# A streaming encoder layer on one core: scores of two heads in turns, a block's closing carried into the next block, stage buffers in another order

## The chip, the cores and the metric

The kernel runs on one core of one Trainium2 chip. The metric is device microseconds of one execution. Five engines work side by side, each through its own list of instructions in order: TensorE (PE, matrix products; its weight loads are counted apart as PEld), VectorE (DVE), ScalarE (ACT), GpSimd (POOL), and SyncE (SP), which here only issues transfers. Matrix products land in PSUM, eight banks, from which DVE or ACT must copy ("evict") them; the other tiles live in SBUF.

## The reference

One layer of an encoder, width 1024, for 2048 prompt tokens and 32 sample tokens. Each of three parts is wrapped as `x = x + rmsnorm(part(rmsnorm(x)))`:

1. one projection `h @ w_in`, whose columns feed a band attention with 8 heads (each 64-token chunk sees itself and 8 chunks before it) and a gated linear attention with 4 heads, key width 64 and value width 128; both outputs go through `w_o`;
2. cross-attention, 4 heads of 256, to 256 memory tokens;
3. a feed-forward block of width 2816.

The lines that matter here:

```
ob, sp = gla_recurrence(qb, kb, vb, la, s0, GLA_BLOCK)   # 4 heads, decay per key channel
def swiglu(h, w_gate, w_up, w_down):
    return (jax.nn.silu(h @ w_gate) * (h @ w_up)) @ w_down
```

## The kernel before

Matrix products are done to near float32 precision with two-part operands: a value is split into a rounded part (`ACT.copy` to float32r, line 77) and a remainder (a subtraction on DVE or POOL, line 81), and a product takes three matmuls (`mm3`, line 136). Projections and the gate and up products use a scheme with seven instead of eight block products (`seven_mov`, `seven_sta`); X, Y and Z are its three output banks.

The program is written in stages, each in its own set of pools: the projections (to about 625 us), attention and linear attention with the output projection (to about 1590), cross-attention (to about 2030), and the feed-forward stage (to the end). SBUF addresses follow the order in which a stage opens its pools, so a new stage's tile must wait until the tiles of the stage before at the same addresses are no longer used.

**What sets the order.** The code names engines and data. A planner then orders every engine's instructions: it goes through a simulated time and gives a free engine the ready instruction with the lowest number. The number is the place in the program text, less an offset inside `tc.high_priority(offset=...)`. `PRI` is 4000; weights are loaded and split at `PRI`. The order is then fixed, and an engine that waits holds all behind it.

**Linear attention (`gla_tile`).** One tile of 128 tokens at a time, 16 tiles and one of 32 sample tokens. Per pair of heads `f`, exponentials of the decays are put into `W`; then each head `e` of the pair (partitions 0 to 63 or 64 to 127) gets 15 products of 64x64 in one PSUM bank (`sps`, lines 922 and 926; the profile calls it `g_s`), which ACT (927) and DVE (928) evict. Two banks (`pm`) serve all of linear attention. The 15 products of a head are issued together, then its eviction, then the next head.

**Cross-attention.** Five blocks of 416 tokens. `mem_out` multiplies by `w_mo` into `y`, `mem_fin` closes: statistic, scaling by `g_post_mem` (1347), residual (1348), write to `x2d`, a second statistic, scaling by `g_pre_ffn` (1352), write to `h2d`. For the last block `mem_fin` runs at twice `PRI`, and the residual's additions alternate between POOL and DVE.

**Feed-forward stage.** Three blocks `b`, each with two column halves `ci` of 348 or 346 tokens. `ffn_raw` loads the input `hr` from `h2d`, `ffn_ops` makes the seven operands `mf` (in `mps[0..6]`). A block has 11 groups `g`. `gate_up(g)` makes two units, gate and up, of seven products with 12 matmuls each, and the result `u`; `down([g-1])` follows, 16 products of 6 matmuls, half 1 first, added by DVE into `acc[ci]` (1510, 183). `acc` has two buffers, `u` three, `sg` five, the output banks `pd` six. In group 8 the next block's input is loaded, in group 10 its operands are made. After group 10, `finish(ci)` closes each half: statistic (1534), Ln and Exp on ACT (85, 86), eight multiplications on DVE (1541), eight residual additions on POOL (183), two loads (1525) and two writes (1544). Both calls stand at the end of the block, ahead of the next block's text:

```
down([NF // 2 - 1], [held])
for ci in (1, 0):
    finish(ci, lambda kh: stage(f"x2r{b}_{ci}_{kh}"))
```

The evictions of `unit` and `down` have no priority of their own; in the projection stage a helper `out` gives evictions twice `PRI`.

Of the kernel before, what the change touches and what calls it, by code (L numbers as in the profile page):

```python
# [45 lines left out]
def encoder_step(ctx, tc, ins, outs):  # L46
# [171 lines left out]


    lo_set[0] = [POOL, DVE]  # L220
    WCH = 1056
    with ExitStack() as ph:
# [136 lines left out]

        def out(f, *a):  # L360

            with tc.high_priority(offset=2 * PRI):
                f(*a)
# [236 lines left out]
    with ExitStack() as ph:  # L600
# [257 lines left out]
        def gla_tile(tk, n, st, name):  # L858
# [53 lines left out]
            for f in range(2):  # L912
                W = Ws[f]
                for e in range(2):
                    h = 2 * f + e
                    rs = slice(e * 64, e * 64 + 64)
                    kf, qf = kq[rs, f, 0], kq[rs, f, 1]
                    ms = gp.tile([P, 7, 64], F32, tag="ms", name=f"{name}_ms{h}")
                    sps = pm.tile([P, 8, 64], F32, tag="gla", name=f"{name}_s{h}")
                    at = at_p[h]  # L920
                    if n == P:
                        PE.matmul(sps[0:64, 7, :], lhsT=W[rs, 1, 0:64], rhs=W[rs, 1, 64:128], start=True, stop=True)
                        for li in range(7):
                            for bk in (slice(0, 64), slice(64, 128)):
                                lh, rh = (W[rs, 2 + li, bk], W[rs, 2 + li, bk]) if li < 6 else (kf[:, bk], qf[:, bk])
                                PE.matmul(sps[bk, li, :], lhsT=lh, rhs=rh, start=True, stop=True)
# [7 lines left out]
                    else:  # L934
                        for li in range(6):
                            lh, rh = (W[rs, 3 + li, :n], W[rs, 3 + li, :n]) if li < 5 else (kf[:, :n], qf[:, :n])
                            PE.matmul(sps[:n, li, :n], lhsT=lh, rhs=rh, start=True, stop=True)
# [278 lines left out]
    with ExitStack() as ph:  # L1216
# [121 lines left out]
        def mem_fin(b, y):  # L1338
            s, n = CB[b]
            last = b == len(CB) - 1  # L1340
            with tc.high_priority(offset=2 * PRI if last else 0):
# [15 lines left out]
        out = []  # L1357
        for b in range(len(CB)):
            mo, heads = mem_attn(b)
            fill = [partial(mem_q, b + 1, mv, m) for m in range(KT)] if b + 1 < len(CB) else out  # L1360
# [4 lines left out]
            out = mem_out(b, mo)  # L1365
            if b != len(CB) - 2:
                for it in out:
                    it()
# [5 lines left out]
    with ExitStack() as ph:  # L1374
# [88 lines left out]
        for b, (s, n) in enumerate(CF):  # L1463
# [219 lines left out]
```

## Time and profile before

| | |
|---|---|
| median of 3 runs | 3535.33 us (3531.69 to 3543.06) |
| profiled execution | 3536.25 us |
| its span | 3534.5 us |
| PE busy | 3254.4 us (92%) |
| DVE, ACT, POOL busy | 2279.1, 1699.5, 1528.3 us |
| mean granted TensorE clock | 0.951 |

Span is the time from the first to the last instruction; the profiled execution lies some microseconds around it. Busy times are sums over the span; an engine's busy matmul time includes matmuls at a lowered clock. In the timeline a row gives start, length, engine, line, operation, tiles written and read, and the number of instructions merged; a bracket gives the idle time before it and what ended it. In rows of groups the two numbers behind the bar are busy time and the mean of one in nanoseconds. Rows of waits give the total, the number of times and the longest. A merged row of overlapping matmuls ends when the last one does.

### The profile page before, as it was taken

The numbers are of one execution on the slowest core, as the hardware profiler recorded it, in microseconds if no ns is written. First come the engines' busy times: TensorE is split into PE (matmuls) and PEld (weight loads), VectorE is DVE, ScalarE is ACT, GpSimd is POOL, SyncE is SP. The second block draws the span as 40 slices with busy tenths as digits, with TensorE's granted clock in tenths as the row PEclk, the third lists the DMA queues.
The fourth block names the chain that finished last, engine by engine and source line by source line (L and its number), as shares of the span: only waits on it lengthen the run. The fifth ranks groups of instructions, "written<-read, shape, count | busy, mean of one in ns | idle before, by whom it ended". The sixth has DMA issues, their size and how long they took to land.

```text
span 3534.5 us, 58393 instructions
## 1 busy us (share of the span) xinstructions
PE 3254.4 (92%) x21387; PEld 3092.7 (87%) x21387; DVE 2279.1 (64%) x4089; ACT 1699.5 (48%) x3716; POOL 1528.3 (43%) x1331
## 2 busy tenths in 40 slices
PE   7788899899999798879999879999989999899998
PEld 7787899788888577879899869999889999899998
DVE  6774855575676666265566766666876666866665
ACT  4554545556665465345455443333443334443334
POOL 4543533353445544653434453333453334543332
PEclk8999999999999798999999979999999999999999
DMA  5448364877585565963655552222342222322222
GB/s 140 155 129 284 105 185 132 260 233 230 177 276 169 188 190 176 295 210 120 212 190 178 155 159 80 72 72 72 94 136 83 72 72 84 100 86 82 72 72 89
DMA packets 520112, 520.42 MB, mean 147 GB/s; under 512 B 81936, under 2 KB 450745, under 8 KB 519825
## 3 DMA queue, kind: packets, MB, share of 16 engines
q1 hardware_dynamic: 519825, 516.70, 47.2%
q8 instruction: 168, 2.75, 0.3%
q14 instruction: 119, 0.97, 0.1%
HBM read 386.82 MB, written 130.87 MB: 146 GB/s over the span
## 4 chain that ended last, share of the span: by engine, by line
PE 64%; DVE 9%; DMA 6%; POOL 3%; ACT 3%; issue 2%; SPq 1%; POOLq 0%; DVEq 0%; ACTq 0%
PE pdn L136 13%; PE pg_X L136 7%; PE pu_X L136 6%; PE wops L989 4%; PE mops L136 4%; PE pg_Y L136 3%; PE pu_Y L136 3%; PE po L715 2%; PE mqps L136 2%; PE pg_Z L136 2%; PE pu_Z L136 2%; PE s L710 1%; PE ms L136 1%; PE pt L742 1%; PE mpv L136 1%
## 5 line engine op out<-in xcount | busy, mean ns | idle before, releaser
L136 PE MATMUL pdn<-u,wd 128*128 128x346 f32 (+1 forms) x3168 | 527.9, 324 | 11.3 <-DVE up L183 9.8
L136 PEld LDWEIGHTS pdn<-u,wd 128*128 128x128 f32 x3168 | 512.0, 191 | 13.8 <-DVE up L183 10.4
L77 ACT CAST wg_s<-wg_r 128x512 fp32r<-128x512 f32 x231 | 139.6, 620 | 420.7 <-PE pdn L136 194.1
L136 PE MATMUL pu_X<-mf,wu_s 128*128 128x346 f32 (+1 forms) x1584 | 280.7, 323 | 11.4 <-DVE up L183 11.4
L136 PE MATMUL pg_X<-mf,wg_s 128*128 128x346 f32 (+1 forms) x1584 | 283.9, 329 | 7.7 <-DVE mf L81 3.3
L183 DVE TENSOR_TENSOR acc<-acc,pdn 128x346 f32<-128x346 f32 (+1 forms) x464 | 231.4, 512 | 87.3 <-PE pdn L136 87.2
L136 PEld LDWEIGHTS pg_X<-mf,wg_s 128*128 128x128 f32 x1584 | 265.0, 195 | 10.5 <-DVE mf L81 4.2
L136 PEld LDWEIGHTS pu_X<-mf,wu_s 128*128 128x128 f32 x1584 | 258.2, 190 | 12.2 <-issue 12.2
L81 POOL TENSOR_TENSOR wu_s<-wu_r,wu_s 128x512 fp32r<-128x512 f32 x132 | 175.9, 1333 | 212.7 <-ACT wu_s L77 208.5
L81 POOL TENSOR_TENSOR wg_s<-wg_r,wg_s 128x512 fp32r<-128x512 f32 x99 | 136.2, 1376 | 292.9 <-ACT wg_s L77 292.9
L989 PE MATMUL wops<-om,wo_s 128*128 128x512 f32 (+1 forms) x960 | 217.9, 378 | 23.9 <-ACT wo_s L77 10.3
L81 POOL TENSOR_TENSOR u<-sg,u 128x346 fp32r<-128x346 f32 (+1 forms) x132 | 135.4, 1037 | 193.1 <-ACT u L77 193.1
L136 PE MATMUL mops<-mo,wmo_s 128*128 128x416 f32 x960 | 199.0, 359 | 14.4 <-ACT mo L1318 6.5
L989 PEld LDWEIGHTS wops<-om,wo_s 128*128 128x128 f32 x960 | 163.8, 204 | 53.3 <-ACT wo_s L77 11.1
L136 PEld LDWEIGHTS mops<-mo,wmo_s 128*128 128x128 f32 x960 | 179.6, 191 | 20.4 <-ACT mo L1318 7.5
L77 ACT CAST wu_s<-wu_r 128x512 fp32r<-128x512 f32 x231 | 136.4, 618 | 70.7 <-DVE wu_r L183 36.0
L715 PE MATMUL po<-prt,v 128*128 128x128 f32 x1120 | 161.9, 290 | 7.9 <-ACT prt L744 5.6
L136 PE MATMUL mqps<-m,wmq_s 128*128 128x416 f32 x768 | 163.1, 362 | 5.1 <-DVE wmq_s L81 5.1
L715 PEld LDWEIGHTS po<-prt,v 128*128 128x128 f32 x1120 | 149.0, 203 | 15.8 <-ACT prt L744 6.3
L81 DVE TENSOR_TENSOR wg_s<-wg_r,wg_s 128x512 fp32r<-128x512 f32 x132 | 97.9, 742 | 90.5 <-ACT wg_s L77 89.1
L136 PEld LDWEIGHTS mqps<-m,wmq_s 128*128 128x128 f32 x768 | 145.0, 194 | 8.5 <-DVE wmq_s L81 5.8
L136 PE MATMUL pg_Y<-mf,wg_s 128*128 128x346 f32 (+1 forms) x792 | 139.5, 325 | 8.9 <-ACT mf L77 5.7
(478 smaller groups left out, 7964.2 us busy)
## 6 DMA issues: line engine op xcount, KB each, us to landing
wg_r<-in_w_ffn_gate_dram SPq DMA_DIRECT2D x66, 512.0 KB, 4.3
wu_r<-in_w_ffn_up_dram SPq DMA_DIRECT2D x66, 512.0 KB, 4.1
wd_r<-in_w_ffn_down_dram SPq DMA_DIRECT2D x66, 512.0 KB, 3.4
wmq_r<-in_w_mq_dram SPq DMA_DIRECT2D x80, 256.0 KB, 2.9
wmo_r<-in_w_mo_dram SPq DMA_DIRECT2D x80, 256.0 KB, 3.1
q<-qd SPq DMA_DIRECT2D x32, 512.0 KB, 5.4
wo_r<-in_w_o_dram SPq DMA_DIRECT2D x64, 256.0 KB, 4.3
om<-od SPq DMA_DIRECT2D x24, 512.0 KB, 7.3
```

Of the source, the lines that this page charges most:

```text
L77: ACT.copy(hi, src)
L81: lo_eng.tensor_tensor(out=lo, in0=src, in1=hi.bitcast(F32), op=ALU.subtract)
L136: PE.matmul(ps, lhsT=a, rhs=b, start=first and i == 0, stop=last and i == len(seq) - 1, skip_group_check=skip)
L183: eng.tensor_tensor(out=out, in0=a, in1=b, op=ALU.add)
L710: PE.matmul(ps_out, lhsT=q[:, 2 * i + e, q0 : q0 + nq], rhs=ks[:, e, k0 : k0 + ncol], start=i == 0, stop=i == 1)
L715: PE.matmul(po[:, e * P : e * P + n], lhsT=v[:kk, j, e * 64 : e * 64 + P], rhs=prt[:kk, j, :n], start=j == 0, stop=j == len(rows) - 1)
L742: PE.transpose(ptp[:kk, j, :n], pr[:n, c0 : c0 + kk], ident[:n, :n])
L989: PE.matmul(ps, lhsT=a, rhs=b, start=i == 0, stop=i == len(seq) - 1)
```

## The change

Three edits. In `gla_tile` the 15 products of the two heads of a pair are issued in turns, head by head within each product, into two banks; the evictions of both follow. In the feed-forward stage all evictions of `unit` and `down` go through `out` (twice `PRI`), which moves to where all stages see it, and `finish` of a block that is not the last is no longer called at its end but kept in `late`: half 1 is closed behind `gate_up(0)` of the next block, half 0 behind `gate_up(1)`. At the change from cross-attention the last `mem_fin` loses its priority, `ffn_raw(0)` and `ffn_ops(0)` get `PRI`, and the feed-forward pools are opened in another order, raw and split weights in pools of their own (`cwr`, `cws`), so that other tiles lie over those of cross-attention. No arithmetic is added or removed.

```diff
-                for e in range(2):
-                    h = 2 * f + e
-                    rs = slice(e * 64, e * 64 + 64)
-                    kf, qf = kq[rs, f, 0], kq[rs, f, 1]
+                hs = [(2 * f + e, slice(e * 64, e * 64 + 64), pm.tile([P, 8, 64], F32, tag="gla", name=f"{name}_s{2 * f + e}")) for e in range(2)]
+                if n == P:
+                    for h, rs, sps in hs:
+                        PE.matmul(sps[0:64, 7, :], lhsT=W[rs, 1, 0:64], rhs=W[rs, 1, 64:128], start=True, stop=True)
+                    for li in range(7):
+                        for bk in (slice(0, 64), slice(64, 128)):
+                            for h, rs, sps in hs:
+                                lh, rh = (W[rs, 2 + li, bk], W[rs, 2 + li, bk]) if li < 6 else (kq[rs, f, 0, bk], kq[rs, f, 1, bk])
+                                PE.matmul(sps[bk, li, :], lhsT=lh, rhs=rh, start=True, stop=True)
...
+                for h, rs, sps in hs:
                     ms = gp.tile([P, 7, 64], F32, tag="ms", name=f"{name}_ms{h}")
...
         def mem_fin(b, y):
             s, n = CB[b]
             last = b == len(CB) - 1
-            with tc.high_priority(offset=2 * PRI if last else 0):
+            if True:
...
-        mps = {i: pool(f"cm{i}", 1) for i in (5, 6)}
+        mps = {i: pool(f"cm{i}", 1) for i in (5, 6, 4)}
         gp = pool("cg", 4)
-        wp = pool("cw", 4)
+        wr = pool("cwr", WRB)
+        mps.update({i: pool(f"cm{i}", 1) for i in (0, 1)})
+        up_ = pool("cp", 3)
+        sp = pool("cs", 4)
+        mps.update({i: pool(f"cm{i}", 1) for i in (3, 2)})
+        ws = pool("cws", WSB)
+        np_ = pool("cn", 1)
         uu = pool("cu", UB)
-        sp = pool("cs", 4)
-        mps.update({i: pool(f"cm{i}", 1) for i in (4, 0, 1, 2, 3)})
-        up_ = pool("cp", 3)
-        np_ = pool("cn", 1)
         xp = pool("cx", 2)
...
             prod(X, w[0], m[0], True, True)
-            ACT.copy(cp[0], X)
+            out(ACT.copy, cp[0], X)
...
             prod(Y, w[3], m[3], False, True)
-            add(DVE, dst[0, 1], cp[2], Y)
+            out(add, DVE, dst[0, 1], cp[2], Y)
...
-        ops = ffn_ops(0, ffn_raw(0))
+        with tc.high_priority(offset=PRI):
+            ops = ffn_ops(0, ffn_raw(0))
+        late = []
...
                         if gs[0] == 0:
-                            DVE.tensor_copy(acc[ci][:, m, :n], ps[:, :n])
+                            out(DVE.tensor_copy, acc[ci][:, m, :n], ps[:, :n])
                         else:
-                            add(DVE, acc[ci][:, m, :n], acc[ci][:, m, :n], ps[:, :n])
+                            out(add, DVE, acc[ci][:, m, :n], acc[ci][:, m, :n], ps[:, :n])
...
                 u = gate_up(g, last and g == NF // 2 - 1)
+                if late:
+                    late.pop(0)()
...
                 down([NF // 2 - 1], [held])
-                for ci in (1, 0):
-                    finish(ci, lambda kh: stage(f"x2r{b}_{ci}_{kh}"))
+                late = [partial(finish, ci, lambda kh, nm=f"x2r{b}_{ci}": stage(f"{nm}_{kh}")) for ci in (1, 0)]
```

More of the change, by code (lines that the diff above doesn't have):

```diff
@@ L217, in seven_sta, with out @@
         put(a22)
+    def out(f, *a):
+        with tc.high_priority(offset=2 * PRI):
+            f(*a)
     lo_set[0] = [POOL, DVE]
@@ L1356, in encoder_step @@
         mv = mem_h(1)
-        out = []
+        proj = []
         for b in range(len(CB)):
             mo, heads = mem_attn(b)
-            fill = [partial(mem_q, b + 1, mv, m) for m in range(KT)] if b + 1 < len(CB) else out
+            fill = [partial(mem_q, b + 1, mv, m) for m in range(KT)] if b + 1 < len(CB) else proj
             for it in weave(heads, fill, lead=QLEAD):
@@ L1364, in encoder_step @@
                 mv = mem_h(b + 2)
-            out = mem_out(b, mo)
+            proj = mem_out(b, mo)
             if b != len(CB) - 2:
-                for it in out:
+                for it in proj:
                     it()
@@ L1428, in put @@
                 def put(q):
-                    w = wp.tile([P, 2, HK, P], F32R, tag="wsp", name=f"{name}_s{len(ops)}", bufs=WSB)
+                    w = ws.tile([P, 2, HK, P], F32R, tag="wsp", name=f"{name}_s{len(ops)}", bufs=WSB)
                     split(w[:, 0], w[:, 1], raw[q])
@@ L1528, in spare, with finish @@
                 return mps[i].tile([P, KT, 348], F32, tag="mov", name=name)
-            def finish(ci, xrs):
+            def finish(ci, xrs, b=b, s=s, n=n, acc=acc, ssqs=ssqs, last=b == len(CF) - 1, load_x2=load_x2):
                 a = acc[ci]
```

33 lines of the change are left out of this document (13 added, 20 removed).

## The prediction

> **What bounds the kernel now.** I read the page first: its busy times, the slices and the chain of work that ended last.
>
> ```profile
> span 3534.5 us, 58393 instructions
> PE 3254.4 (92%) x21387; PEld 3092.7 (87%) x21387; DVE 2279.1 (64%) x4089; ACT 1699.5 (48%) x3716; POOL 1528.3 (43%) x1331
> PE   7788899899999798879999879999989999899998
> PEclk8999999999999798999999979999999999999999
> PE 64%; DVE 9%; DMA 6%; POOL 3%; ACT 3%; issue 2%; SPq 1%; POOLq 0%; DVEq 0%; ACTq 0%
> ```
>
> PE is the bound, and what it can still give lies in the dips of its row. I therefore asked next for the busy time of each engine in stretches cut at the stage changes: the linear-attention stage, the passage from cross-attention to the feed-forward blocks, a quiet part of a feed-forward block, and the two places where one feed-forward block follows another. The columns are stretch, length, busy time (instructions) of PE, PEld, DVE, ACT and POOL, then granted clock, DMA share and GB/s.
>
> ```profile
> 625.00:1590.00 965.00, 861.76 (x6798) 752.01 (x6795) 593.84 (x1551) 538.79 (x1421) 462.80 (x541) 0.92 0.69 219
> 2030.00:2110.00 80.00, 51.53 (x235) 46.75 (x236) 57.60 (x67) 34.64 (x56) 44.28 (x24) 0.77 0.52 166
> 2110.00:2490.00 380.00, 380.00 (x2391) 380.00 (x2391) 230.72 (x389) 147.43 (x291) 142.56 (x117) 1.00 0.25 76
> 2490.00:2620.00 130.00, 112.12 (x655) 109.75 (x654) 115.81 (x144) 64.89 (x113) 72.74 (x50) 0.92 0.43 131
> 2978.00:3108.00 130.00, 112.30 (x655) 109.93 (x654) 115.80 (x145) 65.01 (x114) 72.24 (x50) 0.92 0.36 109
> ```
>
> In the quiet part PE never rests: 380/2391 = 0.159 us per matmul. At that rate the 655 matmuls of each block change need 104.1 us, and take 130: 25.9 us lost, twice. The 235 of the passage need 37.3 us and take 80: 42.7 us lost. Together 94.5 us; nothing is to be had inside a block.
>
> **The change, part by part.**
>
> *Evictions put first (`out` in `unit` and `down`).* In the quiet part there is no idle PE to remove, so they are worth nothing there; at a block change PE's waits and timeline show what they meet.
>
> ```profile
> PE pu_Z L136 <- ACT wu_s L77: 6.4, 1, 6.4
> PE pu_X L136 <- DVE up L183: 5.7, 1, 5.7
> PE pdn L136 <- DVE up L183: 4.9, 1, 4.9
> 2511.06 6.97 PE L136 MATMUL pdn<-u,wd 128*128 128x348 f32 x24 [4.93 <-DVE up L183]
> 2554.22 6.12 DVE L1541 SCALAR_TENSOR_TENSOR acc<-acc,g_post_ffn,n_r 128x348 f32<-128x348 f32 x6 [2.34 <-ACT n_r L86]
> 2579.98 8.73 DVE L1541 SCALAR_TENSOR_TENSOR acc<-acc,g_post_ffn,n_r 128x348 f32<-128x348 f32 x8 [2.25 <-ACT n_r L86]
> 2588.64 0.50 DVE L183 TENSOR_TENSOR up<-pu_c,pu_Y 128x346 f32<-128x346 f32 x1
> ```
>
> Three stops, 17.0 us. In two of them DVE works through a run of the closing's multiplications (6.12 and 8.73 us, 1.09 each) while an eviction (`up`) or a weight's subtraction stands behind; in the first it prepares the next block's input. The rest of the 25.9 us is clock: after the 4.93 us stop, 24 matmuls took 6.97 us where 0.159 each makes 3.8, so 3.2 us more. The Trainium skill ("TensorE: Matmul & The Clock Gate", Part 1) says that a window of about 3.4 us without work halves the clock and as long a busy one restores it. The trace agrees in kind; by the page's figures a stop would cost only 1.7 us beyond itself, and the sum below would be 3 us lower.
>
> With evictions ahead of everything, what stands before one is a single running instruction, about 2 us at most.
>
> *The closing moved (`late`).* Nothing is added or removed: per column half one statistic matmul, ACT's Ln and Exp with their table loads, 8 DVE multiplications, 8 POOL additions, two loads and two writes. But the half 1 closing now ranks behind group 0 of the next block, half 0's behind group 1, and the next block's `acc` buffers (two, one per half) are the ones being closed. What is late next is therefore the first write of `acc`, in the first `down`. From the end of the old block PE has groups 0 and 1 (168 matmuls each, 26.7 us), half 1 of `down` (48, 7.6 us) and six banks of half 0 (36, 5.7 us): 66.7 us, then it stands. Half 0's closing, step by step:
>
> ```profile
> 2575.53 0.75 PE L1534 MATMUL n_ps<-ssq,ones 128*128 128x348 f32 x2
> 2576.30 1.28 ACT L85 ACT_TABLE_LOAD   x1
> 2579.45 0.50 ACT L86 ACTIVATE n_r<-n_r 128x348 f32<-128x348 f32 x1
> 2587.15 5.91 POOL L183 TENSOR_TENSOR acc<-acc,x2r 128x348 f32<-128x348 f32 x5
> out_dram<-acc SPq DMA_DIRECT2D x6, 692.0 KB, 4.6
> ```
>
> If its matmul gets a place only when group 1 ends (53.4 us): 0.75 + 3.65 (ACT, 2576.30 to 2579.95) + 8.73 + 1.2 (last addition) + 4.6 (write) gives 72.3, a stop of 5.6 us. If DVE, 61% busy in the quiet part (230.72 of 380), leaves it only the other 39%, 8.73 becomes 22.4 and the stop 19.3. With 3.2 us of clock the new loss is 9 to 22.5 us; it is nothing if the matmul finds an earlier gap. I take 15, nearer the middle of the first two, since a PE that must stand also empties DVE's list. Saved: 11 per change, **22 us** for both; bounds 52 (no stop at all) and -3 (22.5 with the first stop of 4.9 left as it is makes 27.4 where 25.9 stood). The loads and writes also move in SP's queue: a write that waits for POOL's addition holds the weight loads behind it. The four raw buffers cover that, two units or 26.7 us of PE; without this cover PE would stand for the difference.
>
> *The stage change laid out anew.* Now the feed-forward stage starts so:
>
> ```profile
> 2026.22 3.48 PE L136 MATMUL mops<-mo,wmo_s 128*128 128x416 f32 x10 [3.01 <-POOL wmo_s L81]
> 2030.43 0.40 SPq L1401 DMA_DIRECT2D hr<-h2d  x1
> 2037.73 0.66 PE L136 MATMUL pg_X<-mf,wg_s 128*128 128x348 f32 x1 [1.23 <-ACT mf L77]
> 2047.59 0.66 PE L136 MATMUL pg_Y<-mf,wg_s 128*128 128x348 f32 x1 [4.67 <-ACT mf L77]
> 2067.18 0.95 PE L136 MATMUL pu_Z<-mf,wu_s 128*128 128x348 f32 x2 [4.47 <-ACT wu_s L77]
> 2077.19 0.86 PE L99 MATMUL n_ps<-n_acc,ones 128*128 128x416 f32 x2
> 2079.70 8.12 DVE L1352 SCALAR_TENSOR_TENSOR y<-y,g_pre_ffn,n_r 128x416 f32<-128x416 f32 x8 [1.34 <-ACT n_r L86]
> 2081.04 7.12 SPq L1353 DMA_DIRECT2D h2d<-y  x8
> h2d<-y SPq DMA_DIRECT2D x40, 208.0 KB, 2.1
> ```
>
> Cross-attention's last matmul ends at 2029.7; the input `hr` is asked for only at 2030.43, and for 60 us PE waits for its operands in turn, while DVE and POOL also close cross-attention (`mem_fin`, priority 8000 ahead). After the change the input ranks 4000 ahead, and its buffers lie, by the tile sizes summed in pool order, over the memory keys and values, free when the attention heads end; the first two operands lie over the query buffers, the next over `mo` and the old weights, free at 2029.7. Four of the eight split-weight buffers lie over block 3's `y`, in use until its last write. So PE can go on at about 2030. What then is late is `mem_fin` of the last block, no longer ahead: `u` and `acc` lie over its scratch (`bn`) and its `y` (`bx0`). Today the scratch's last statistic is read at 2077 and `y` is written by 2081.04 + 7.12 + 2.1 = 2090. Without `u`, the five `sg` buffers let PE do group 0 (26.7 us), six products of the next gate (72 matmuls, 11.4 us) and some 10 us of its `up` half: until about 2078. If `mem_fin` keeps its pace, PE stops for some 4 us and 39 are saved; if it is 25 us later, PE stands 23 us, then 5 more for `acc` and 3 for the clock, and 12 are saved. The early preparation must also pass through DVE under cross-attention's end:
>
> ```profile
> L81 DVE TENSOR_TENSOR mf<-hr,mf 128x1384 fp32r<-128x1384 f32 x10 | 18.9, 1894 | 0.5 <-ACT mf L77 0.5
> L180 DVE TENSOR_TENSOR hr<-hr,hr 128x1384 f32<-128x1384 f32 x8 | 16.9, 2112 | 0.1
> ```
>
> Two splits and three differences before 2030 are 2 x 1.89 + 3 x 2.11 = 10.1 us ahead of `mops` evictions; three output banks hide most of it, and if they hide none, 12 becomes 2. Between the bounds 39 and 2 I take **22 us**, for a `mem_fin` about 10 us later. Extra table loads, as Silu and Ln/Exp now alternate, fall on an ACT busy 34.64 of 80 us.
>
> *Scores of two heads in turns.* 15 matmuls of 64x64 per head, recorded twice each; here heads 0 and 1 of a tile, as issued now one after the other, then the evictions' and waits' rows.
>
> ```profile
> 884.92 0.85 PE L926 MATMUL g_s<-g_W 64*64 64x64 f32 x22
> 885.56 0.27 PE L922 MATMUL g_s<-g_W 64*64 64x64 f32 x1
> 885.60 0.22 PE L926 MATMUL g_s<-g_kq 64*64 64x64 f32 x1
> 886.63 4.00 PE L989 MATMUL wops<-om,wo_s 128*128 128x512 f32 x16
> L928 DVE TENSOR_TENSOR g_ms<-g_s,gmask x64: 609/625/626, 670.9 to 1393.6; 128x448 f32<-128x448 f32 x64
> PE g_s L922 <- DVE g_ms L928: 11.3, 6, 5.8
> PEld g_s L922 <- DVE g_ms L928: 13.3, 8, 6.1
> ```
>
> A head's records start 0.63/21 = 0.030 us apart (884.92 to 885.55), two heads take 1.8 us. Head 1's first record (L922, 885.56) starts before head 0's last ones (the `g_kq` product, from 885.60), so the two halves of the array do run together where the order lets them. Perfect overlap would halve 1.8 us: 0.9 saved at most, I take 0.8, times 32 pairs = 26 us of PE time. PE is busy 861.76 of 965 us in this stage, so not all of it reaches the end; I take half, **13 us**. Bounds: 26, and -11, since both banks must now be free together and the 11.3 us of waits could double. The Trainium skill ("TensorEngine Tiling (Array Packing)", Key Properties) says that different tiles of the array load weights and multiply in parallel; its section PSUM Bottleneck speaks against the gain: after the speed-up the copy out of PSUM may set the pace. The 4.00 us of other matmuls between two pairs are longer than the pair's 2 x 0.625 us of DVE, so I leave that to a rival.
>
> *The sum.* The profiled execution took 3536.25 us (span 3534.5 and 1.75 around it), 0.9 above the median of 3535.33. 3536.25 - 13 - 22 - 22 = **3479 us**, 1.6% faster.
>
> **The rivals.** (a) Both covers hold: the closings find gaps and `mem_fin` keeps its pace, 13 + 39 + 52 = 104: 3432. For it: DVE has 39% free inside a block. Against: the rank behind two whole groups. (b) DVE's evictions of the paired scores set their pace and PE stands for two banks: no gain, and 11 us more waits, 3479 + 13 + 11 = 3503. By the page's PSUM rule this is the case; the 4.00 us row is against it. (c) The closing does not spread: the order still holds eight multiplications in one run, only later, and 25.9 us are lost again each time: 3479 + 22 = 3501. For it: nothing in the code separates them. Against: evictions now outrank them. (d) On the other side: the wait for `acc` half 0 replaces all. It decides from 35/2 = 17.5 us beyond today's 25.9, a loss of 43.4 us per block change, that is with `acc` free 107 us (66.7 + 43.4 - 3.2) after the old block ends instead of 72 to 86; at a loss of 55 the time is 3536 - 35 + 58 = 3559. For it: rank behind group 1 on PE, DVE, POOL and SP alike. Against: once PE stands, no new evictions come to pass it.
>
> **How the numbers follow.** 0.3% (11 us) is about what a measurement of this kernel can tell from no change. Forecast 0.48, with its own range 3447 to 3510; (a) 0.14, (b) 0.12, (c) 0.08, (d) 0.13, gains and losses cancelling to within 0.3% 0.05. Faster: 0.48 + 0.14 + 0.12 + 0.08 = 0.82; same 0.05; slower 0.13. The range, 3432 to 3530, reaches from (a) past (b) and (c); it leaves out (d) and the half of (a) that would go below, 0.20.
>
> **What would show it.** Right: score records of a pair interleaved, the pair in about 1.0 us; `hr` asked for before 2000, first `pg_X` at about 2030 and no wait of `mf`; at a block change no wait of PE for `up` behind a run of multiplications, but one of `acc` for a write or POOL. Wrong: a first `down` standing over 20 us for `acc`; cross-attention's matmuls later than now by the preparation's 10 us; a `mem_fin` that ends after 2115; pairs not interleaved, because a bank was not free when the order was made.

## The result and the profile after

The changed kernel takes 3520.74 us (median of 4 runs, 3519.66 to 3523.07), the kernel before, run beside it, 3535.86 (3531.69 to 3543.06): a ratio of 0.9958, 95% interval 0.9946 to 0.997. That is 15 us faster (11 to 19) where 57 were forecast. The profiled execution took 3519.91 us. The page after, its span, the engines' busy times, the slices of PE and its clock:

```profile
span 3518.1 us, 58416 instructions
PE 3230.3 (92%) x21387; PEld 3070.5 (87%) x21387; DVE 2258.6 (64%) x4089; ACT 1705.1 (48%) x3719; POOL 1541.9 (44%) x1331
PE   7788899899999799879999879999989999899998
PEclk8999999899999799989999989999999999999999
```

The dips are where they were. The stretches that the prediction cut, moved to the same places of the work (the passage begins at cross-attention's last matmul, a block change where as many feed-forward matmuls have run); columns as before:

```profile
625.00:1590.00 965.00, 849.03 (x6812) 742.85 (x6811) 601.34 (x1555) 542.95 (x1430) 467.33 (x543) 0.92 0.70 221
2020.00:2100.00 80.00, 54.83 (x279) 49.67 (x280) 65.31 (x76) 40.44 (x69) 41.91 (x27) 0.83 0.48 155
2100.00:2470.00 370.00, 370.00 (x2323) 370.00 (x2322) 220.15 (x383) 143.32 (x282) 147.06 (x116) 1.00 0.26 78
2473.00:2603.00 130.00, 112.31 (x658) 109.51 (x657) 116.70 (x145) 65.14 (x115) 74.48 (x50) 0.93 0.43 131
2961.00:3091.00 130.00, 112.43 (x659) 109.69 (x659) 116.38 (x144) 65.20 (x115) 74.79 (x50) 0.93 0.36 109
```

Count the matmuls. The passage does 279 in 80 us instead of 235: 44 more, 7.0 us at 0.159 each, where 22 were forecast. The block changes do 658 and 659 in 130 us instead of 655: half a microsecond each, where 11 each were forecast. This count (matmuls in the first 130 us of the first block change) is the measure in the experiments below; at 0.159 a full 130 us would hold 818, so 655 means 25.9 us lost and 658 means 25.4.

**Block change.** PE's waits of the changed kernel in 2473 to 2603, then rows of the timelines of PE and DVE there:

```profile
PE pu_Y L136 <- ACT wu_s L77: 6.9, 1, 6.9
PE pdn L136 <- DVE acc L183: 4.0, 2, 3.3
PE pu_X L136 <- DVE up L183: 3.9, 1, 3.9
PE pdn L136 <- DVE up L183: 2.4, 1, 2.4
```

```profile
2519.75 8.96 PE L136 MATMUL pdn<-u,wd 128*128 128x348 f32 x55
2544.13 0.75 PE L1540 MATMUL n_ps<-ssq,ones 128*128 128x348 f32 x2
2548.34 8.46 DVE L1547 SCALAR_TENSOR_TENSOR acc<-acc,g_post_ffn,n_r 128x348 f32<-128x348 f32 x8 [2.26 <-ACT n_r L86]
2557.77 0.75 PE L1540 MATMUL n_ps<-ssq,ones 128*128 128x348 f32 x2
2558.08 0.50 DVE L183 TENSOR_TENSOR up<-pu_c,pu_Y 128x346 f32<-128x346 f32 x1
2562.44 3.35 PE L136 MATMUL pu_X<-mf,wu_s 128*128 128x346 f32 x12 [3.93 <-DVE up L183]
2572.19 8.05 DVE L1547 SCALAR_TENSOR_TENSOR acc<-acc,g_post_ffn,n_r 128x348 f32<-128x348 f32 x8 [3.24 <-ACT n_r L86]
2583.65 3.57 PE L136 MATMUL pu_Y<-mf,wu_s 128*128 128x346 f32 x11 [6.87 <-ACT wu_s L77]
2599.80 0.94 DVE L222 COPY acc<-pdn 128x346 f32<-128x346 f32 x2
```

The old block ends at 2528.71 (first row). Both runs of eight multiplications are there, 8 to 10 us later in the new block than before, and behind each a stop of PE (3.9 and 6.9 us; the matmuls of one `pu_Y` end at 2550.92, and its eviction stands behind the first run until 2558.08). The four rows come to 17.2 us; before, three came to 17.0. The wait for `acc` that the prediction feared is not there: the second run is over at 2580.24, the first copy into `acc` is at 2599.80.

**Passage.** Rows of PE, DVE, SP and ACT of the changed kernel at the end of cross-attention:

```profile
1986.29 0.43 SPq L1405 DMA_DIRECT2D hr<-h2d  x1
2017.00 2.56 PE L136 MATMUL mops<-mo,wmo_s 128*128 128x416 f32 x11
2018.74 10.35 DVE L1354 SCALAR_TENSOR_TENSOR y<-y,g_pre_ffn,n_r 128x416 f32<-128x416 f32 x8 [0.68 <-ACT n_r L86]
2019.42 10.02 SPq L1355 DMA_DIRECT2D h2d<-y  x8
2031.14 0.62 ACT L77 CAST wg_s<-wg_r 128x512 fp32r<-128x512 f32 x1 [0.91 <-DMA h2d<-y]
2031.81 4.09 PE L136 MATMUL pg_X<-mf,wg_s 128*128 128x348 f32 x12 [12.26 <-ACT wg_s L77]
```

The input is early, as forecast (asked for at 1986.29), and PE no longer waits for its operands `mf`. But PE stands 12.26 us for the first split weight, whose rounding on ACT waits for a write `h2d<-y`. In the built program this weight lies at 151296, over `y` of cross-attention's block 3 (151040 to 164352), and that block's closing (from 2018.74, its last write issued at 2029.44) ends behind cross-attention's last matmul (2019.56).

**Scores.** Busy time on the tile `g_s` alone in 625 to 1590 (length, then PE, PEld, DVE, ACT) before:

```profile
625.00:1590.00 965.00, 74.61 (x1920) 66.72 (x1920) 39.87 (x64) 12.39 (x64) 0.92 0.69 219
```

and after, with PE's wait for its bank there:

```profile
625.00:1590.00 965.00, 68.30 (x1920) 60.67 (x1920) 39.83 (x64) 11.64 (x64) 0.92 0.70 221
```

```profile
PE g_s L917 <- DVE g_ms L933: 6.9, 3, 5.6
```

6.3 us of PE time are saved where 26 were forecast. PE also waits less for a bank than before (6.9 us for the 11.3 that the prediction shows). In the order that was made only 12 of the 32 pairs of full tiles alternate, most of these in part; the others run one head after the other as before. Both heads read the same tile `W`, so by the planner's rule head 0's products were issued alone because head 1 had no bank yet.

A caution for what follows: the last output projection of the linear-attention stage ends between 1498.3 and 1504.8 in the 13 profiles that share the changed kernel's scores, so a stage's gain of a few microseconds is read from more than one run.

### The profile page after: what moved, and what is told of

It is laid out like the page before. It is cut to its first block, busy times and chain, and to the rows that moved or that the text cites. A ratio compares the mean times of both kernels' runs of the same rounds, so it can differ in the third digit from the quotient of the medians.

```text
span 3518.1 us, 58416 instructions
## 1 busy us (share of the span) xinstructions
PE 3230.3 (92%) x21387; PEld 3070.5 (87%) x21387; DVE 2258.6 (64%) x4089; ACT 1705.1 (48%) x3719; POOL 1541.9 (44%) x1331
## 4 chain that ended last, share of the span: by engine, by line
PE 62%; DVE 11%; DMA 5%; ACT 3%; issue 3%; POOL 2%; SPq 1%; DVEq 0%; POOLq 0%; ACTq 0%
PE pdn L136 13%; PE pg_X L136 6%; PE pu_X L136 6%; PE mops L136 5%; PE wops L991 4%; PE pu_Y L136 3%; PE pg_Y L136 3%; PE po L715 2%; PE mqps L136 2%; PE pu_Z L136 2%; PE pg_Z L136 2%; PE s L710 1%; PE ms L136 1%; DVE y L1349 1%; PE mpv L136 1%
## 5 line engine op out<-in xcount | busy, mean ns | idle before, releaser
L81 POOL TENSOR_TENSOR u<-sg,u 128x346 fp32r<-128x346 f32 (+1 forms) x132 | 151.9, 1161 | 236.0 <-ACT u L77 236.0
L715 PEld LDWEIGHTS po<-prt,v 128*128 128x128 f32 x1120 | 147.5, 200 | 14.8 <-ACT prt L744 4.8
L136 PE MATMUL pu_Y<-mf,wu_s 128*128 128x346 f32 (+1 forms) x792 | 141.3, 327 | 14.3 <-ACT wu_s L77 14.3
```

Source lines behind the costliest of these rows:

```text
L81: lo_eng.tensor_tensor(out=lo, in0=src, in1=hi.bitcast(F32), op=ALU.subtract)
L136: PE.matmul(ps, lhsT=a, rhs=b, start=first and i == 0, stop=last and i == len(seq) - 1, skip_group_check=skip)
L715: PE.matmul(po[:, e * P : e * P + n], lhsT=v[:kk, j, e * 64 : e * 64 + P], rhs=prt[:kk, j, :n], start=j == 0, stop=j == len(rows) - 1)
```

## The experiments

Times "below" are from the ratio to the kernel before, times 3535.

**One part alone.** Scores only:

```
+ for li in range(7):
+     for bk in (slice(0, 64), slice(64, 128)):
+         for h, rs, sps in hs:
+             PE.matmul(sps[bk, li, :], lhsT=lh, rhs=rh, start=True, stop=True)
...
```

> The kernel before with only the scores issued in turns. Theory now, from the trace after the change: most pairs were not interleaved, because the order that was made issues head 0's ready products while head 1's bank is not yet free; the linear-attention stage still ends some 9.5 us earlier (end of the output projections 1510.0 before, 1498.8 after, less 1.8 us that was there before the stage). So 8 to 11 us below the kernel before, about 3526 us, and PE's time on g_s in 625:1590 near 68 us as in the trace after, where it was 74.6 before. The prediction's theory: 13 us, 3522 to 3523. A rival, that the stage's gain comes from elsewhere in the change: less than 3 us.

3525.2 us against 3533.77, ratio 0.9979 (0.9971 to 0.9988): 7 us (4 to 10). The time of `g_s` is nearly that of the whole change:

```profile
625.00:1590.00 965.00, 69.08 (x1920) 61.46 (x1920) 39.86 (x64) 11.66 (x64) 0.91 0.70 221
```

So the gain of this stage is the scores' own. Closing only:

```
- ACT.copy(cp[0], X)
+ out(ACT.copy, cp[0], X)
...
- for ci in (1, 0):
-     finish(ci, lambda kh: stage(f"x2r{b}_{ci}_{kh}"))
+ late = [partial(finish, ci, lambda kh, nm=f"x2r{b}_{ci}": stage(f"{nm}_{kh}")) for ci in (1, 0)]
```

> The kernel before with only the evictions put first and the closing moved behind groups 0 and 1 of the next block. Theory now: the eight multiplications of a closing stay in one run wherever they are put, so PE still stands some 17 us at each block change; 0 to 3 us below the kernel before, about 3534 us. The prediction's theory: 22 us, 3514. A rival, that the closing gains by itself but something else in the whole change took it away again: 10 us or more below.

3533.41 us, ratio 1.0002 (0.9993 to 1.0011): nothing. The count at the block change is 658, as in the whole change:

```profile
2484.00:2614.00 130.00, 111.96 (x658) 109.11 (x657) 117.00 (x144) 65.16 (x115) 74.65 (x50) 0.93 0.42 131
```

Stage change only:

```
- mps = {i: pool(f"cm{i}", 1) for i in (5, 6)}
+ mps = {i: pool(f"cm{i}", 1) for i in (5, 6, 4)}
...
+ ws = pool("cws", WSB)
...
- ops = ffn_ops(0, ffn_raw(0))
+ with tc.high_priority(offset=PRI):
+     ops = ffn_ops(0, ffn_raw(0))
```

> The kernel before with only the stage change: buffers in the new order, the first block's input 4000 ahead, cross-attention's closing no longer ahead. Theory now: the first split weight of the gate lies over block 3's y, and waits until that is written (about 12 us of PE standing before the first pg_X); 4 to 8 us below the kernel before, about 3530 us, and the wait of pg_X for wg_s is there at 10 us or more. The prediction's theory: 22 us, 3514. A rival, that the passage gains fully only without the evictions put first: 12 us or more below.

3532.1 us, ratio 0.9998 (0.9989 to 1.0007): nothing that can be told, 4 us faster at most. The passage does 260 matmuls in its first 80 us, 25 more than before, and the wait is there:

```profile
2026.00:2106.00 80.00, 52.98 (x260) 48.29 (x261) 65.95 (x77) 40.42 (x68) 41.90 (x28) 0.83 0.47 155
```

```profile
PE pg_X L136 <- ACT wg_s L77: 16.4, 2, 13.2
```

The parts alone give 7 us, the whole 15. To see whether that is measurement, the changed kernel was run once more:

> The changed kernel itself once more, beside the three that are built upon it and the kernel before. The three parts alone gave 7.4 us (scores), nothing (closing) and nothing (stage change), the whole change 15. Theory that the parts add up and the first comparison came out high: 5 to 9 us below the kernel before. Theory that the parts need each other: 12 to 17 us below.

3518.57 us against 3533.29, ratio 0.9959 (0.9945 to 0.9974): 15 us again. And it was run with the scores put back, that is closing and stage change together:

> The changed kernel with the scores issued one head after the other as before, so the closing and the stage change together. Theory that these two need each other (evictions put first let the early preparation pass without delay): 5 to 9 us below the kernel before, as the whole gave 15 and the scores alone 7. Theory that they give nothing, as alone, and the scores gain more in company: within 3 us of the kernel before.

3532.79 us against 3532.8, ratio 0.9995 (0.9986 to 1.0005): 2 us (-2 to 5), though its passage, with 270 matmuls in 80 us, is nearly as quick as the whole change's. By the times, 7 and 2 against 15 leave 6 us open; the intervals (4 to 10, -2 to 5, 11 to 19) allow for them only at their ends. The profiles settle most of it. The last output projection of the linear-attention stage ends at 1507.9 to 1512.9 in the four profiles with the scores as before and at 1498.3 to 1504.8 in the 13 with the changed kernel's: 9.8 us on average. From cross-attention's last matmul to the end of the span, the two profiles with neither closing nor stage change take 1504.8 and 1505.5 us, the four with both and nothing more in that stage 1498.5 to 1501.7: 4.7 us on average. So the scores are worth some 10 us and the other two together some 5, near the upper ends of their intervals, and nothing says that the parts help each other.

**All pairs in turns.** In the changed kernel the 28 further products of a pair were issued behind both heads' first product, so that the turns begin only when both banks are held:

```
- PE.matmul(sps[0:64, 7, :], lhsT=W[rs, 1, 0:64], rhs=W[rs, 1, 64:128], start=True, stop=True)
+ pr_ = PE.matmul(sps[0:64, 7, :], lhsT=W[rs, 1, 0:64], rhs=W[rs, 1, 64:128], start=True, stop=True)
...
+ with tc.issue_after(pr_.ins):
+     PE.matmul(sps[bk, li, :], lhsT=lh, rhs=rh, start=True, stop=True)
```

> The changed kernel, with the 28 further products of a pair issued behind both heads' first product, so that both banks are held before the turns begin and every full pair is interleaved (29 switches between heads instead of 1 in most pairs). Theory now (the gain of a pair is real, the order did not take it): a pair takes about 1.0 us instead of 1.85 in the 20 pairs that are not yet in turns, 16 us less PE time on g_s (68 to about 52 us), of which about half reaches the end: 5 to 10 us below the changed kernel, about 3513 us. A rival, that the order was right to go one after the other since the second bank comes late: PE's time on g_s falls, but the waits of g_s for g_ms grow by as much, 3519 to 3525 us. A third, that two heads in turns do not run together on the array: PE's time on g_s stays at 68 us or more.

3530.93 us, ratio 0.9995 (0.9986 to 1.0004): some 13 us slower than the changed kernel. That is the second theory in kind, but slower than the 3519 to 3525 it gave. One pair in the timeline of PE, then the time on `g_s` and the wait for its bank:

```profile
892.38 0.32 PE L917 MATMUL g_s<-g_W 64*64 64x64 f32 x2
...
894.87 0.27 PE L917 MATMUL g_s<-g_W 64*64 64x64 f32 x1
...
894.98 0.85 PE L923 MATMUL g_s<-g_W 64*64 64x64 f32 x44
...
895.68 0.33 PE L923 MATMUL g_s<-g_kq 64*64 64x64 f32 x6
```

```profile
625.00:1590.00 965.00, 53.27 (x1920) 44.60 (x1920) 39.89 (x64) 9.91 (x64) 0.90 0.69 218
```

```profile
PE g_s L917 <- DVE g_ms L934: 19.6, 8, 8.8
```

From head 1's first product (894.87) to the last (896.01) is 1.14 us, near the 1.0 forecast, and PE saves 21.3 us on `g_s` (74.61 to 53.27), near the 26. None of it reaches the end: the stage's last output projection ends at 1509.5, as before (1510.0). The stage must now hold both of its two banks at once (here head 1's first product comes 2.5 us after head 0's), and the wait for them is 19.6 us for 6.9 in the changed kernel. What PE saves on `g_s` over the changed kernel (68.30 to 53.27) it stands idle: its busy time in this window falls by 14.5 us (849.03 to 834.56), at one length. Why the kernel is then slower than the changed one, and not level, is not shown; the granted clock over the stage is 0.90 for 0.92. The Trainium skill ("TensorEngine Tiling (Array Packing)", Gotcha 1: PSUM Pressure) says that row tiles write to different banks and so raise the pressure on PSUM. The trace agrees, with these 19.6 us.

**The run of eight.** In the changed kernel the closing was cut into 16 steps, each issued behind one DVE eviction or product of the next block's groups 0 and 1:

```
...
+ def step(after):
+     if late:
+         with tc.issue_after(after.ins):
+             if next(late[0], 1):
+                 late.pop(0)
...
- out(add, DVE, dst[0, 1], cp[2], Y)
+ turn(dst[0, 1], cp[2], Y)
```

> The changed kernel with the closing cut into 16 steps (one multiplication and one addition each), each issued behind one DVE eviction or product of the next block's groups 0 and 1. Theory now (the run of eight multiplications is what PE waits for): the waits of pu_X for up (3.9 us) and of pu_Y for wu_s (6.9 us) go, and with them some 3 us of clock each; the preparation of the next input (3.9 us with pdn waiting for up) stays. 10 to 14 us per block change, 20 to 28 in all, so 3493 to 3500. A rival, that the steps behind evictions make the evictions wait in turn or the first down stand for acc: less than 6 us, or slower than the changed kernel, with a wait of pdn for acc in the stretch 60 to 90 us after the old block.

3517.12 us against 3533.29, ratio 0.995 (0.9938 to 0.9963), the changed kernel beside it 0.9959: 3 us lower by the ratios, within the intervals. The multiplications now come one or two at a time, the waits of 6.9 and 3.9 us are gone, and six of 0.9 to 1.9 us stand in their place. The window and the largest of these:

```profile
2477.00:2607.00 130.00, 116.87 (x677) 113.36 (x676) 116.64 (x145) 66.67 (x116) 75.77 (x51) 0.93 0.40 120
```

```profile
PE pu_X L136 <- DVE up L1456: 1.9, 1, 1.9
```

677 for 658 is 3 us per change, not the 10 to 14 expected: a run broken up is not a run hidden, while DVE is at work 116.64 of 130 us as before. What the closing costs at all was therefore asked by leaving parts out. Without its multiplications:

```
- DVE.scalar_tensor_tensor(out=a[:, k, :n], in0=a[:, k, :n], ...)
+ if last:
+     DVE.scalar_tensor_tensor(out=a[:, k, :n], in0=a[:, k, :n], ...)
```

> The changed kernel with the closing's multiplications by gain and norm left out where one block follows another (the output of the first two blocks is then unscaled); all else stays, POOL's additions too. Theory that the run of eight is what PE waits for: the waits of pu_X (3.9 us) and pu_Y (6.9 us) go with their clock, and those of the preparation stay; 10 to 14 us per change, 3491 to 3499. Theory that DVE's whole work is the bound: 16 products at 1.03 us are 16.5 us of DVE, and PE loses up to as much less: 14 to 18 per change, 3483 to 3491. A rival, that the loads of x2r and the writes on SP's queue make the weights late: 5 us or less in all.

3503 us against 3534.24, ratio 0.9911 (0.9897 to 0.9924), some 17 us below the changed kernel: less than either theory gave, more than the rival. Without POOL's additions:

```
- add(DVE if last and k % 2 else POOL, a[:, k, :n], a[:, k, :n], xr[:, kk, :n])
+ if last:
+     add(DVE if k % 2 else POOL, a[:, k, :n], a[:, k, :n], xr[:, kk, :n])
```

> The changed kernel with POOL's additions of the residual left out at the closing where one block follows another (the first two blocks' output then lacks the residual). Theory that DVE's multiplications are slow because POOL adds beside them (1.03 us against a least of 0.57): a run of eight falls from 8.4 to about 4.6 us and the two waits of 3.9 and 6.9 to nothing and 3: 6 to 10 us per change, 3499 to 3507. A rival, that their duration does not come from POOL: runs of 8 us stay and the time is within 4 us of the changed kernel.

3506.61 us, ratio 0.9917 (0.9904 to 0.9931), some 15 us below, as the first theory had it; the runs of eight take 5.06 and 4.02 us for 8.46 and 8.05. The two windows, products out and then additions out:

```profile
2473.00:2603.00 130.00, 118.91 (x707) 115.22 (x707) 112.51 (x141) 65.97 (x117) 75.77 (x53) 0.96 0.42 131
```

```profile
2476.00:2606.00 130.00, 119.96 (x708) 117.09 (x708) 114.55 (x158) 66.90 (x117) 56.77 (x37) 0.95 0.40 131
```

Either gives back about 8 us per change (49 or 50 matmuls), no more. That the additions alone are worth as much as the multiplications shows how the two are tied where the multiplications come in a run. The multiplications' group in 2490 to 2620 of the changed kernel and of the one without additions (busy, then mean in ns):

```profile
L1547 DVE SCALAR_TENSOR_TENSOR acc<-acc,g_post_ffn,n_r 128x348 f32<-128x348 f32 x16 | 16.5, 1101 | 5.5 <-ACT n_r L86 5.5
```

```profile
L1547 DVE SCALAR_TENSOR_TENSOR acc<-acc,g_post_ffn,n_r 128x348 f32<-128x348 f32 x16 | 9.1, 636 | 3.4 <-ACT n_r L86 3.4
```

**The preparation of the next input.** It stops PE too (the waits of `pdn`, 6.4 us). In the changed kernel its differences were cut in two, so that an eviction waits for half as long an instruction:

```
+ halves = lambda eng, o, a, c: [sub(eng, o[:, k : k + 2], a[:, k : k + 2], c[:, k : k + 2]) for k in (0, 2)]
...
- seven_mov(raw, put)
+ seven_mov(raw, put, halves)
```

> The changed kernel with only the differences of the feed-forward input cut into two pieces each. Theory now (an eviction, though put first, waits for the whole instruction that DVE is at, and those differences last 4 us beside POOL's work): the waits of pdn for acc and up at the preparation (6.4 us) halve; 2 to 4 us per block change with the clock, 3510 to 3514. A rival, that DVE's work as a whole sets the pace at a block change (88.6 of 100 us busy from 2490 to 2590) and smaller pieces alter nothing: within 3 us of the changed kernel.

3517.06 us against 3534.24, ratio 0.995 (0.9937 to 0.9964); the count is 661. The two waits of `pdn` become 5.0 and 0.8 us, 5.8 for 6.4: within 3 us or so of the changed kernel, the rival. Then the preparation was left out:

```
- if g == NF // 2 - 3:
-     raw = ffn_raw(b + 1)
...
- ops = ffn_ops(b + 1, raw)
+ ops = [tuple(x[:, :, : CF[b + 1][1]] for x in o) for o in ops]
```

> The changed kernel with the preparation of the next block's input left out (blocks 1 and 2 use block 0's operands again, so most of their output is wrong; four loads, seven splits and five differences per block change are not done). The preparation holds DVE some 22 us per change (five differences at 2.1 to 4.6 us, five remainders at 1.89). Theory that DVE's whole work sets the pace at a block change: 9 to 13 us less per change, 3493 to 3501, more than its own stops of 6.4 us. Theory that only single stops count: 6.4 us and the clock behind them, 6 to 9 per change, 3501 to 3507. A rival, that the rest is weights that come late: 3 or less per change.

3502.03 us against 3532.8, ratio 0.9916 (0.9903 to 0.9929), some 15 us below the changed kernel, 7.5 per change: the theory of single stops. And with the closing's multiplications left out as well:

> The changed kernel without the preparation and without the closing's products at the two block changes (as the two runs that left out one of them). Theory that DVE's whole work sets the pace: the 25 us lost per change nearly vanish, 18 to 24 less per change, 3471 to 3484. If the two only add: the sum of the two single gains, 15 us from the products and that of the run without the preparation. If something else holds the rest, such as the weights or the statistic's sums: 15 or less per change, 3490 or more.

3491.72 us, ratio 0.9878 (0.9861 to 0.9895): 28 us below the changed kernel, 14 per change. The windows, preparation out and both out:

```profile
2471.00:2601.00 130.00, 118.75 (x710) 117.38 (x709) 100.34 (x149) 58.81 (x111) 65.53 (x51) 0.95 0.35 109
```

```profile
2477.00:2607.00 130.00, 122.31 (x751) 119.08 (x750) 93.05 (x137) 62.29 (x117) 67.45 (x54) 1.00 0.37 116
```

52 matmuls for the one, 49 for the other, 93 for both: the two nearly add up. The theory that DVE's whole work sets the pace (18 to 24 us per change) does not hold, and something else holds a part, as the third expectation had it. The bill of a block change reads: 25.4 us lost, 14.8 of them (93 matmuls at 0.159) the closing's multiplications and the preparation together, some 8 for either alone, and 10.6 that remain without both. What these 10.6 are was not settled; PE's named waits there are 7.5 us, the largest 3.2 for ACT's copies.

**The first weight.** In the changed kernel the closing of cross-attention's block 3 was put ahead:

```
- if True:
+ with tc.high_priority(offset=2 * PRI if b == len(CB) - 2 else 0):
```

> The changed kernel with the closing of cross-attention's block 3 put 8000 ahead (the changed kernel has it at 0), so that block 3's y, over which the first split weights of the feed-forward stage lie, is written before cross-attention ends. Theory now: pg_X then starts within 3 us after the last matmul of cross-attention instead of 12.3 us, and most of that reaches the end: 6 to 10 us below the changed kernel. A rival, that the weight was late for other reasons (its subtraction on DVE, POOL, ACT) or that what goes ahead delays the output projection's evictions by as much: less than 3 us.

3517.42 us against 3533.29, ratio 0.9953 (0.9941 to 0.9966), the changed kernel beside it 0.9959: 2 us by the ratios, within the intervals, where 6 to 10 were expected. PE's first rows of the feed-forward stage:

```profile
2016.62 4.38 PE L136 MATMUL mops<-mo,wmo_s 128*128 128x416 f32 x22 [1.04 <-DVE wmo_s L81]
2020.84 2.09 PE L136 MATMUL pg_X<-mf,wg_s 128*128 128x348 f32 x12
2028.31 0.94 PE L136 MATMUL pg_X<-mf,wg_s 128*128 128x348 f32 x2 [3.47 <-ACT wg_s L77]
```

The wait of 12.26 us is gone, so its cause is shown. But the next weights are late in their turn (3.47 us here). What the first 80 us gain (328 matmuls instead of 279, 7.8 us) shows in this profile, of the fastest of the five executions (1490.5 us from cross-attention's last matmul to the end, for 1498.5 and 1500.2 in the two profiles of the changed kernel), and hardly in the times.

**Together.** Closing in steps, block 3 ahead, differences in halves:

> The changed kernel with the closing in 16 steps, block 3's closing ahead, and the differences of the feed-forward input cut into two pieces of 2 x 348 each, so that an eviction waits for half as long a one. If the first two add up and the third takes away half of the 3.9 us of pdn waiting for up at a block change: 30 to 40 us below the changed kernel, about 3485. If the third does nothing: the sum of the other two.

3504.59 us against 3533.29, ratio 0.9919 (0.9906 to 0.9932): 29 us below the kernel before, 14 below the changed kernel where 30 to 40 were expected and the single ratios (0.0009, 0.0006, 0.0009) add to 8. The count at the block change is 697: steps and halves together give 39 matmuls where they gave 19 and 3 alone, which suggests that one stop hid behind another. With the first copies into `acc` on ACT:

```
- out(DVE.tensor_copy, acc[ci][:, m, :n], ps[:, :n])
+ out(ACT.copy, acc[ci][:, m, :n], ps[:, :n])
```

> The kernel with the closing in 16 steps, block 3's closing ahead and the differences in halves (3504.6 before), and the first down's copies of its sums into acc done by ACT instead of DVE: 16 copies of 0.5 us, 8 us of DVE per block, of which the first two blocks' stand beside the spread closing. Theory that DVE's work is the bound at a block change: 3 to 8 us below, 3497 to 3502. A rival, that DVE has room again by the time of the first down: within 3 us of 3504.6.

3504.35 us against 3534.24, ratio 0.9915 (0.9901 to 0.9928): no change, the rival. Instead of that, with the closing's additions on DVE:

```
- add(DVE if last and k % 2 else POOL, a[:, k, :n], a[:, k, :n], xr[:, kk, :n])
+ add(DVE if not last or k % 2 else POOL, a[:, k, :n], a[:, k, :n], xr[:, kk, :n])
```

> The kernel with the closing in 16 steps, block 3's closing ahead and the differences in halves (3504.6 before), and the closing's additions of the residual on DVE instead of POOL. Theory that the two engines hold each other up (a multiplication lasts 0.64 us without POOL's additions and 1.10 with them): DVE's work stays the same, 0.64 + 0.51 for 1.10, and POOL loses 19 us of work per change, 2 to 8 us below. A rival, that DVE's count of instructions is what counts: 16 more of 0.5 us per change, 5 to 10 us above.

3502.64 us against 3532.8, ratio 0.9913 (0.9899 to 0.9927): level with 0.9919, 31 us below the kernel before. Its median is the lowest of the versions that leave nothing out, but the intervals of the last three overlap. The multiplications' group in 2490 to 2620 of the kernel without this edit (3504.59 us), then the two groups of this one:

```profile
L1560 DVE SCALAR_TENSOR_TENSOR acc<-acc,g_post_ffn,n_r 128x348 f32<-128x348 f32 x16 | 13.8, 879 | 0.2 <-ACT n_r L86 0.2
```

```profile
L1560 DVE SCALAR_TENSOR_TENSOR acc<-acc,g_post_ffn,n_r 128x348 f32<-128x348 f32 x16 | 12.9, 831 | 0.0
L183 DVE TENSOR_TENSOR acc<-acc,x2r 128x348 f32<-128x348 f32 x16 | 10.0, 646 | 0.0
```

The theory's premise did not hold here: with the closing in steps a multiplication lasts 0.879 us beside POOL's additions already, and 0.831 without them, not 1.10 and 0.64. So DVE does some 9 us more per change (12.9 and 10.0 for 13.8), and the block change does 696 matmuls for 697. That this work costs nothing that can be told speaks once more against DVE's whole work as the bound; the gain of 2 to 8 us that the theory gave is not shown.

## Why the prediction was right or wrong

**The bound: right.** PE is the bound, the quiet part has nothing to give, and the losses lie at the places named.

**The block changes: wrong, 22 us forecast, 1 in the profile and none in the times.** The step that failed is "With evictions ahead of everything, what stands before one is a single running instruction, about 2 us at most." A priority acts while the order is made, in the planner's time. By its rule the evictions cannot have been due there when the multiplications were (the planned times are not on record). So eight stand in a row in DVE's list, and on the chip an eviction that comes due earlier cannot pass them. This was rival (c), given 0.08: "nothing in the code separates them", and the row of 8.46 us shows it. Two more assumptions fell. A lower rank did not delay the closing by two groups: half 0's statistic, put at 53.4 us after the old block, ran at 2557.77, 29 us after it (31 before the change: 2575.53 less 2544.7), so the wait for `acc`, and rival (d) with it, never came. And the prize was smaller than the bill: the 25.9 us were all put to stops that the move could end, while leaving the multiplications out altogether gives back only 8 per change. One reading was off too: during most of the first stop of the kernel before (4.93 us) DVE is not at the next input but at the remainder of a down weight (2506.97 to 2510.58, 3.61 us), while POOL makes a remainder of that input (2505.56 to 2510.03). And the clock's 3.2 us were read behind that one stop, where the granted clock is 0.50 for 6 us; behind the stops of 3.9 and 6.9 us in the changed kernel it is 0.50 for some 3.

**The passage: wrong in size, 22 us forecast, 7.0 in its window.** The input was early as forecast, and `mem_fin` of the last block kept its pace (its last write is issued 59 us after cross-attention's last matmul, 2079.0 less 2019.56; before 58, 2088.2 less 2029.7). By the prediction's own working 39 us should then have been saved. The step that failed is "Four of the eight split-weight buffers lie over block 3's `y`, in use until its last write. So PE can go on at about 2030": the overlap was seen, and no price was put on it. Cross-attention now ends at 2019.56, the last of the writes is issued at 2029.44 (2019.42 + 10.02), and one of the four buffers is the first that the gate fills, with all later ones behind it. The sign "first `pg_X` at about 2030" came true (2031.81) by luck: cross-attention now ends 10 us earlier, and behind it stands the wait of 12.26 us. With that wait removed the window gains 14.8 us in all (328 matmuls for 235), still less than 22, since the following weights are late.

**The scores: right in kind, 13 us forecast, 7 (4 to 10) measured, some 10 by the stage's end in the profiles.** The term "I take 0.8, times 32 pairs = 26 us of PE time" was nearly right for pairs in turns (21.3), but only 6.3 of it was taken. The sign named in the prediction ("a bank was not free when the order was made") is what happened. That the stage still gains more than the 6.3 goes with the shorter wait for a bank (11.3 to 6.9), which the prediction put down as a risk only. The other factor, "I take half", was wrong for the pairs that are forced: there none of it reaches the end. Rival (b) had the right thing, two banks that wait, but it comes with the forced pairs and not with the change as it was made.

**The sum.** 13 + 22 + 22 were 57. The ends of the stages in the profiles give 10 for the scores and 5 for the other two, which is the 15 that the times show; the windows of the passage and the block changes give 7.0 and 1, somewhat more than these 5. The sign held, and so did the range, which was wide because it reached from the best case past two rivals; the forecast's own range, 3447 to 3510, did not.

## What to carry to other kernels

A priority shapes an order that is fixed before the run; to keep short, urgent work from standing behind a run of long work, tie the pieces of the run to instructions of the other work, and first measure by leaving the run out what hiding it could bring. When buffers are laid over an older stage's, look at which old tile lies under the first buffer that the new stage fills, since work done in order then waits for that one alone. Time saved on the busiest engine by holding two scarce buffers at once can be lost to the wait for the second.

## What the hardware showed that was not expected

A run of multiplications of two tiles on DVE (128x348) lasts longer while POOL adds tiles: 16.5 us for 16 with the additions and 9.1 without, 1.101 and 0.636 us each. An addition on POOL lasts 1.225 us in both cases, beside the multiplications and in the run that left them out. So here DVE pays and POOL does not. The Trainium skill ("SBUF — State Buffer", Who interferes with whom) says that a DVE instruction with two inputs in SBUF contends with a POOL instruction that reads SBUF, and calls the port that they share an exclusive lock. The trace agrees that the two contend. It does not show one standing still for the whole of the other's recorded time: 0.636 and 1.225 us one after the other would be 1.86 a pair, and POOL's eight additions beside a run of eight took 9.57 us (2550.52 to 2560.09), 1.20 a pair, though spans on POOL are rough. With the closing in steps the multiplications lasted 0.879 us on average beside the additions and 0.831 without.

Products of 64x64 of two heads, one in each half of the array's rows, took 1.14 us for 29 in turns where 30, one head after the other, took 1.8: a gain of some 1.5 and not of two.
